# A hybrid decoder block on one core: 208 gathered tokens instead of 192, and other buffers around them

## The chip, the cores and the metric

The kernel runs on one core of one Trainium2 chip. The time is the device time of one execution in microseconds. PE is TensorE (PEld its weight loads), DVE is VectorE, ACT is ScalarE, POOL is GpSimd, SP is SyncE, whose queue issues the plain transfers; POOL issues the indirect ones (row gathers).

## The reference

512 tokens of width 2048 pass a mixer (projections, a short convolution, attention, two merges, an output projection), and then a feed-forward layer of 16384 experts. Each token has 8 heads; a head scores two tables of 128 keys, keeps 16 of each, and picks 16 of the 256 sums. So a token uses 128 of the 16384 experts:

```
hidden = jnp.einsum("td,thkd->thk", xb, u_table[ib])
act = jax.nn.gelu(hidden, approximate=False) * gb
out = jnp.einsum("thk,thkd->td", act, v_table[ib])
```

`u_table` and `v_table` have 16384 rows of 2048 fp32 numbers. Everything is fp32.

## The kernel before, in words

A matmul is done as three fp32r matmuls (`mm3`, lines 161 to 163): each operand is split in a high part (ACT, line 130) and the rest (DVE, line 131). Weights come in halves of 128x1024: `whalf` loads a raw half with SP (512 KB), ACT makes `whi`, DVE makes `wlo`. There are 1024 such halves. Each is used for 24 matmuls in the projections.

The feed-forward layer is done in two ways at once. The first `G0` = 192 tokens are **gathered**: for each of a token's 128 experts POOL fetches a row of `u` and later one of `v` for 128 partitions at a time (1 MB), and DVE multiplies the row with the normalized tokens `gx` and sums (line 701), or multiplies it with the activation and adds it to a sum (line 708). Tokens 0 to 127 are one segment of 128 slots; tokens 128 to 191 are put on the partitions twice, 64 slots each, and the two sums are added at the end. The other `ND` = 320 tokens are **dense**: all experts are computed for them on PE, with 320 columns per matmul, and the result of `u` is multiplied with a plane of gates (`gd`, `gt`) that is zero where a token did not pick the expert. The planes are made of one-hot rows by fp32 matmuls (`gates`, line 673), 16 tokens to a plane.

Order of the program: mixer and output projection of tokens 0 to 255 (until about 690 us); six projections of the second half; the queries of tokens 0 to 255 (`queries`); the rest of the second half's mixer, its output projection and its queries, until about 1705 us; then the dense stage. That has 16 chunks of 8 tiles: `up` (8 units of 48 matmuls with `uT`) and `down` (the same number with `vT`). `up` of chunks 0 to 7 comes first (`AHEAD`), to 2231 us, its results are kept in DRAM (`hdd`); `down` of chunks 0 to 7 follows, to 2690 us; then `up` and `down` alternate.

`route` (the top-16 searches, DVE) and `gates` run beside this in small steps: after each unit or half unit a generator is moved on by a cost budget (`SIDE_A0`, `SIDE_A`, `SIDE_D`). The gather is moved on by `pump(rate)`, one fetch and one consumption per round; in the later dense stage the rest of the rounds is spread evenly over the units. A fetch also waits for a mark two evictions back. The order on each engine is then fixed by a scheduler, and DVE, ACT, PE and SP each work strictly in that order. The consuming instructions on DVE are pinned in their order.

Four `row` buffers (8 KB a partition) hold the fetched rows, the sum of the `v` rounds (`acc`) and other things; a row is fetched when one is free. In the dense stage there are 4 raw buffers `wraw`, 3 further raw ones in `spare`, and 3 pairs of split halves (`WHL`). `finish_rows` normalizes the finished tokens: two `Square` activations write their unwanted products to a PSUM tile of the kind `z`, of which the down projection uses both.

## Time and profile before

| | us |
|---|---|
| median of 3 runs | 3613.26 |
| lowest, highest | 3609.4, 3621.5 |
| the profiled execution: its time | 3619.12 |
| the profiled execution: its span | 3617.4 |
| PE busy in the span | 3513.1 |
| DVE busy | 2831.2 |
| ACT busy | 1616.3 |

The span runs from the first to the last instruction; the execution's time is 1.7 us longer. A matmul's busy time overlaps the next one's, so PE's pace is read from counts of matmuls in a stretch. DMA share is the mean busy share of the 16 DMA engines.

### The profile page before, as it was taken

To read this page: it belongs to the slowest core of one execution; us is meant where nothing else is said; L and a number is where in the kernel's file an instruction comes from. 1 tells how busy PE (TensorE), PEld (TensorE's weight loads), DVE (VectorE), ACT (ScalarE), POOL (GpSimd) and SP (SyncE) were. 2 spreads that over 40 slices of the span, in tenths; PEclk is the share of its full clock that TensorE was granted. 3 is DMA by queue.
4 is the path that set the end of the run, shared out by engine and by line. 5 is a ranking of instruction groups with operands and counts; after the bars stand their busy time and mean duration, and the time that the engine had idled before them with its cause. 6 is when DMAs were issued, how large, how long until landed. Compare 5 with 4: busy or idle time off the path is not lost.

```text
span 3617.4 us, 63262 instructions
## 1 busy us (share of the span) xinstructions
PE 3513.1 (97%) x25347; PEld 3410.4 (94%) x25347; DVE 2831.2 (78%) x4022; ACT 1616.3 (45%) x2275; POOL 659.3 (18%) x520
## 2 busy tenths in 40 slices
PE   9999999999999999889999999999999999999998
PEld 8999998898888999779999999999999999999998
DVE  6565557559987878788999886888887878888886
ACT  6454445445555534544337773333333333333334
POOL 0000000001233322112131111221122322322220
PEclk9999999999999999999999999999999999999999
DMA  6556555654788889898888889899988988899884
GB/s 204 180 178 225 187 187 196 208 184 137 260 348 309 335 332 346 322 331 335 298 327 319 311 315 365 329 356 338 339 328 328 346 330 333 327 346 343 328 329 162
DMA packets 292920, 1049.29 MB, mean 290 GB/s; under 512 B 35921, under 2 KB 105169, under 8 KB 238673
## 3 DMA queue, kind: packets, MB, share of 16 engines
q1 hardware_dynamic: 237328, 642.56, 50.5%
q0 software_dynamic: 55296, 402.68, 28.7%
q8 instruction: 199, 3.26, 0.4%
q14 instruction: 97, 0.79, 0.1%
HBM read 996.57 MB, written 47.97 MB: 289 GB/s over the span
## 4 chain that ended last, share of the span: by engine, by line
PE 59%; DMA 5%; DVE 4%; issue 2%; ACT 1%; POOL 0%; SPq 0%; ACTq 0%; DVEq 0%; POOLq 0%
PE pj L163 10%; PE pj L161 10%; PE pj L162 10%; PE z L161 9%; PE z L162 9%; PE z L163 9%; DVE wlo L131 2%; DMA wraw<-in_w_in 2%; PE pj L673 2%; DMA row<-in_u,idx 1%; DVE row L701 1%; ACT whi L130 1%; PE z L439 1%; DMA row<-in_v,idx 0%; DMA wraw<-in_w_mix 0%
## 5 line engine op out<-in xcount | busy, mean ns | idle before, releaser
L130 ACT ACTIVATE whi<-wraw 128x1024 fp32r<-128x1024 f32 x827 | 874.1, 1059 | 1258.0 <-PE pj L162 723.2
L131 DVE TENSOR_TENSOR wlo<-wraw,whi 128x1024 fp32r<-128x1024 f32 x827 | 1008.3, 1223 | 412.5 <-ACT whi L130 405.6
L161 PE MATMUL pj<-xhi,whi 128*128 128x256 f32 x2560 | 723.5, 283 | 12.5 <-ACT whi L130 10.3
L163 PE MATMUL pj<-xhi,wlo 128*128 128x256 f32 x2560 | 720.4, 283 | 13.5 <-DVE wlo L131 13.4
L162 PE MATMUL pj<-xlo,whi 128*128 128x256 f32 x2560 | 718.1, 281 | 0.0
L161 PE MATMUL pj<-dxhi,whi 128*128 128x320 f32 (+1 forms) x2304 | 710.0, 308 | 4.5 <-ACT whi L130 4.3
L163 PE MATMUL pj<-dxhi,wlo 128*128 128x320 f32 (+1 forms) x2304 | 703.6, 307 | 3.4 <-DVE wlo L131 3.3
L162 PE MATMUL pj<-dxlo,whi 128*128 128x320 f32 (+1 forms) x2304 | 705.2, 306 | 0.0
L161 PE MATMUL z<-ahi,whi 128*128 128x320 f32 x2048 | 632.0, 310 | 3.9 <-ACT z L190 2.9
L162 PE MATMUL z<-alo,whi 128*128 128x320 f32 x2048 | 631.8, 309 | 2.4 <-DVE alo L131 2.4
L163 PE MATMUL z<-ahi,wlo 128*128 128x320 f32 x2048 | 630.6, 309 | 1.8 <-DVE wlo L131 1.8
L163 PEld LDWEIGHTS pj<-xhi,wlo 128*128 128x128 f32 x2560 | 481.6, 189 | 23.6 <-DVE wlo L131 20.9
L161 PEld LDWEIGHTS pj<-xhi,whi 128*128 128x128 f32 x2560 | 482.5, 188 | 21.1 <-ACT whi L130 14.4
L690 POOL DMA_INDIRECT row<-in_v,idx x192 | 292.7, 1525 | 1060.2 <-DVE row L708 429.8
L162 PEld LDWEIGHTS pj<-xlo,whi 128*128 128x128 f32 x2560 | 482.3, 188 | 2.8 <-issue 1.6
L708 DVE SCALAR_TENSOR_TENSOR row<-row,gact 128x2048 f32<-128x2048 f32 x192 | 450.3, 2345 | 27.2 <-DMA row<-in_v,idx 27.2
L701 DVE SCALAR_TENSOR_TENSOR row<-row,gx 128x2048 f32<-128x2048 f32 x192 | 438.3, 2286 | 31.2 <-DMA row<-in_u,idx 31.1
L690 POOL DMA_INDIRECT row<-in_u,idx x192 | 289.0, 1505 | 863.1 <-DVE row L701 239.9
L161 PEld LDWEIGHTS pj<-dxhi,whi 128*128 128x128 f32 x2304 | 434.3, 189 | 5.5 <-ACT whi L130 5.1
L163 PEld LDWEIGHTS pj<-dxhi,wlo 128*128 128x128 f32 x2304 | 432.9, 188 | 5.4 <-DVE wlo L131 5.4
L162 PEld LDWEIGHTS pj<-dxlo,whi 128*128 128x128 f32 x2304 | 434.0, 188 | 0.0
L130 ACT ACTIVATE whi<-spare 128x1024 fp32r<-128x1024 f32 x197 | 208.8, 1060 | 425.4 <-PE z L162 266.9
(232 smaller groups left out, 4979.8 us busy)
## 6 DMA issues: line engine op xcount, KB each, us to landing
wraw<-in_w_in SPq DMA_DIRECT2D x320, 512.0 KB
wraw<-in_uT SPq DMA_DIRECT2D x187, 512.0 KB
wraw<-in_vT SPq DMA_DIRECT2D x128, 512.0 KB
spare<-in_vT SPq DMA_DIRECT2D x128, 512.0 KB
spare<-in_uT SPq DMA_DIRECT2D x69, 512.0 KB
wraw<-in_w_mix SPq DMA_DIRECT2D x64, 512.0 KB
wraw<-in_w_out SPq DMA_DIRECT2D x64, 512.0 KB
wraw<-in_wq SPq DMA_DIRECT2D x64, 512.0 KB
```

The lines of the kernel that those rows point to most:

```text
L130: nc.scalar.activation(hi, src, AF.Copy)
L131: nc.vector.tensor_tensor(lo, src, hi.bitcast(F32), OP.subtract)
L161: nc.tensor.matmul(acc, shi, mhi, start=first, stop=False)
L162: nc.tensor.matmul(acc, shi, mlo, start=False, stop=False)
L163: pe_last[0] = nc.tensor.matmul(acc, slo, mhi, start=False, stop=last)
L439: nc.tensor.matmul(z[:, c], stat.bitcast(F32), src[:, c], start=False, stop=True, skip_group_check=True)
L673: behind(nc.tensor.matmul(gp[:, t * P:t * P + P], oh[:, t, 0], oh[:, t, 1], start=True, stop=True))
L690: ins = nc.gpsimd.indirect_dma_start(out=g, out_offset=None, in_=tab, in_offset=bass.IndirectOffsetOnAxis(ap=idx[0:np_, s:s + 1], axis=0))
L701: pin(nc.vector.scalar_tensor_tensor(g, g, 1.0, gx, OP.mult, OP.mult, accum_out=hid[:, s:s + 1]))
L708: pin(nc.vector.scalar_tensor_tensor(acc[0:np_], g, act[:, s:s + 1], acc[0:np_], OP.mult, OP.add))
```

## The change

Three groups of edits. First, `NG2` goes from 64 to 80: 208 tokens are gathered, in three segments (128 tokens of 128 slots; 64 tokens twice with 64 slots; 16 tokens eight times with 16 slots), 416 rounds instead of 384, and the dense stage has 304 columns and 19 gate planes. The copies of a segment are now added in a tree of transfers and additions. Routing is done for four heads at a time, half 0 of tiles 0 and 1 and then half 1, and the gather starts when the first half's indices are there. Second, the sum of the `v` rounds is kept in `gx`: the first round overwrites it, the last writes to its own row buffer, and the residual `x2d` is loaded and added at the end. So no `row` is held through the `v` rounds, but `gx` is not free for the next segment until the last round. Third, in the dense stage 1 instead of 3 `spare` buffers are left for raw halves (5 raw ones in all instead of 7), and a fourth pair `whi4`, `wlo4` is taken for every fourth half. `rms_scale` now squares 8 pieces of 256 into an SBUF tile.

```
-NG2 = 64
+SEGS = ((0, 0, 128), (1, 0, 64), (1, 64, 16))
+NG2 = 80
-SPB2 = 3
+SPB2 = 1
     def whalf(src):
         turns[0] += 1
-        if spare_ok[0] and turns[0] % 2:
+        if spare_ok[0] and turns[0] % 5 == 0:
             raw = spare()
...
-        hi = wp.tile([P, 1024], F32R, name="whi", bufs=WHL)
-        lo = wp.tile([P, 1024], F32R, name="wlo", bufs=WHL)
+        if spare_ok[0] and turns[0] % (WHL + 1) == 0:
+            hi, lo = (late[2].tile([P, 1024], F32R, name=n, bufs=1) for n in ("whi4", "wlo4"))
+        else:
+            hi, lo = (wp.tile([P, 1024], F32R, name=n, bufs=WHL) for n in ("whi", "wlo"))
...
     def rms_scale(pool, x):
-        ss = pool.tile([P, 2], F32, name="ss", bufs=2)
-        for c in range(2):
-            junk = ztile()
-            nc.scalar.activation(junk, x[:, c * 1024:c * 1024 + 1024], AF.Square, accum_out=ss[:, c:c + 1])
-        return rms_inv(ss)
+        ss = pool.tile([P, 8], F32, name="ss", bufs=2)
+        for c in range(8):
+            junk = pool.tile([P, 256], F32, name="junk", bufs=1)
+            nc.scalar.activation(junk, x[:, c * 256:c * 256 + 256], AF.Square, accum_out=ss[:, c:c + 1])
+        nc.vector.tensor_reduce(ss[:, 0:1], ss, AX.X, OP.add)
+        return rms_root(ss)
...
-    def route(pool, tile_no, st):
+    def route(pool, tile_no, hh, st):
...
             if s == 0:
...
-                acc = row()
-                load_acc(acc)
-            pin(nc.vector.scalar_tensor_tensor(acc[0:np_], g, act[:, s:s + 1], acc[0:np_], OP.mult, OP.add))
+                pin(nc.vector.tensor_scalar(gx, g, act[:, 0:1], None, OP.mult))
+                return
+            pin(nc.vector.scalar_tensor_tensor(g if s == nslot - 1 else gx, g, act[:, s:s + 1], gx, OP.mult, OP.add))
...
+        for tile_no, p0, n in SEGS:
+            R = P // n
...
+            def finish(t):
+                m = P // 2
+                while m >= n:
+                    o = row()
+                    nc.sync.dma_start(o[0:m], t[m:2 * m])
+                    nc.vector.tensor_tensor(t[0:m], t[0:m], o[0:m], OP.add)
+                    m //= 2
                 o = row()
-                nc.sync.dma_start(o[0:NG2], t[r * NG2:r * NG2 + NG2])
-                nc.vector.tensor_tensor(t[0:NG2], t[0:NG2], o[0:NG2], OP.add)
+                nc.sync.dma_start(o[0:n], x2d[rows])
+                nc.vector.tensor_tensor(t[0:n], t[0:n], o[0:n], OP.add)
+                finish_rows(t, rows, final_gain())
...
     def routing(h):
-        for tt in range(2):
-            yield from route(rts[0], 2 * h + tt, st)
+        for hh in range(2):
+            for tt in range(2):
+                yield from route(rts[0], 2 * h + tt, hh, st)
...
-        if st["routes"][0] and what != "half":
+        if st["idx"][0] and what != "half":
```

Place one is DVE in the queries of the first 256 tokens. Before, when half of the scores are searched (`MAX`, `MAX_INDEX`, `MATCH_REPLACE`), twelve `wlo` subtractions follow with nothing between them, and then the next scores:

```order
L550 MATCH_REPLACE ttmp<-ls,row 128x128 x2
L551 MAX ls<-ttmp 128x8 x2
L552 MAX_INDEX ls<-ls,ttmp 128x8 x2
L131 TENSOR_TENSOR wlo<-wraw,whi 128x1024 x12
L548 MAX ls<-row 128x8 x8
```

Now the rest of the routing of four heads stands between the same subtractions (`sv` are the picked sums, `gate` the gates of tile 0):

```order
L133 TENSOR_TENSOR wlo<-wraw,whi 128x1024
L558 MATCH_REPLACE ttmp<-ls,row 128x128
L622 TENSOR_TENSOR spare<-fa,iota 128x1024
L617 TENSOR_SCALAR f_8839<-f_8839 128x64
L558 MATCH_REPLACE ttmp<-ls,row 128x128
L559 MAX ls<-ttmp 128x8
L133 TENSOR_TENSOR wlo<-wraw,whi 128x1024
L624 TENSOR_TENSOR spare<-spare,tif 128x1024
L618 TENSOR_TENSOR fb<-fb,f_8839 128x64
```

Half of two tiles' routing has moved ahead of the scores of the other half; the first consumption of a gathered row stands behind 268 subtractions instead of 289.

Place two is the end of the first segment, tokens 0 to 127, in the dense stage. On DVE, before, the root's steps (L194, L196) have other work between them:

```order
L708 SCALAR_TENSOR_TENSOR row<-row,gact 128x2048
L131 TENSOR_TENSOR wlo<-spare,whi 128x1024
L779 TENSOR_TENSOR hd<-hd,gt 128x320
L194 TENSOR_TENSOR ss<-ss 128x1
L131 TENSOR_TENSOR alo<-hd,ahi 128x320
L196 RECIPROCAL ss<-ss 128x1
L730 SCALAR_TENSOR_TENSOR row<-row,ss 128x2048
L131 TENSOR_TENSOR wlo<-wraw,whi 128x1024
```

Now the residual is added first (L779), and the steps stand closer:

```order
L721 SCALAR_TENSOR_TENSOR row<-row,gact,gx 128x2048
L859 TENSOR_TENSOR dacc<-z,dacc 128x608
L779 TENSOR_TENSOR row<-row 128x2048
L133 TENSOR_TENSOR wlo_28253<-wraw,whi_28252 128x1024
L859 TENSOR_TENSOR dacc<-z,dacc 128x608
L195 TENSOR_REDUCE ss<-ss 128x1
L204 RECIPROCAL ss<-ss 128x1
L746 SCALAR_TENSOR_TENSOR row<-row,ss 128x2048
L795 TENSOR_TENSOR hb<-hb,gt 128x304
L859 TENSOR_TENSOR dacc<-z,dacc 128x608
L133 TENSOR_TENSOR wlo<-wraw,whi 128x1024
```

The place moved from behind 787 subtractions (where `up` of chunk 8 ends and its `down` begins) to behind 747, in the `down` of chunk 6, where the results kept in DRAM are read back beside it (`hb`).

Place three is SP at the end. Now the three transfers of the last segment's tree stand between the last weight loads (before there was one, with 64 rows), and the dense tokens' residual (L903) comes behind the last of them:

```order
L774 DMA row<-row 64x2048
L147 DMA wraw<-in_vT 128x1024 x2
L774 DMA row<-row 32x2048
L147 DMA spare<-in_vT 128x1024
L774 DMA row<-row 16x2048
L778 DMA row<-x2d 16x2048
L740 DMA row<-in_norm_final 128x2048
L147 DMA wraw<-in_vT 128x1024 x2
L740 DMA row<-in_norm_final 128x2048
L147 DMA wraw<-in_vT 128x1024
```

Each of the three waits for the addition before it on DVE, and the loads behind it in the queue wait too.

## Rows read from the trace of the kernel before

**Rows 1.** The page: span and busy time; DMA queues with MB and share.

```profile
span 3617.4 us, 63262 instructions
PE 3513.1 (97%) x25347; PEld 3410.4 (94%) x25347; DVE 2831.2 (78%) x4022; ACT 1616.3 (45%) x2275; POOL 659.3 (18%) x520
q1 hardware_dynamic: 237328, 642.56, 50.5%
q0 software_dynamic: 55296, 402.68, 28.7%
```

**Rows 2.** Busy time by stretch: us, engines with instructions, clock, DMA share, GB/s.

```profile
400.00:500.00 100.00, 100.00 (x851) 100.00 (x850) 57.72 (x72) 42.86 (x53) 0.00 (x0) 1.00 0.56 185
730.00:807.00 77.00, 77.00 (x659) 77.00 (x659) 40.10 (x90) 32.08 (x42) 0.00 (x0) 1.00 0.53 176
1202.00:1277.00 75.00, 74.00 (x617) 72.01 (x616) 60.22 (x63) 34.02 (x42) 21.11 (x14) 1.00 0.95 356
1705.00:2231.00 526.00, 516.84 (x3606) 513.09 (x3605) 459.40 (x1001) 289.62 (x534) 95.38 (x64) 0.99 0.88 322
2231.00:2690.00 459.00, 453.82 (x3076) 450.93 (x3075) 391.85 (x369) 159.57 (x186) 93.36 (x65) 1.00 0.91 338
2690.00:2810.00 120.00, 117.14 (x781) 116.87 (x780) 93.91 (x86) 44.35 (x55) 27.45 (x19) 0.97 0.86 322
2810.00:3541.00 731.00, 730.97 (x4981) 730.28 (x4981) 601.51 (x547) 261.02 (x322) 194.52 (x118) 1.00 0.89 335
3000.00:3100.00 100.00, 100.00 (x684) 100.00 (x683) 78.35 (x82) 34.55 (x44) 25.72 (x16) 1.00 0.86 326
```

**Rows 3.** Groups of the stretch 2810 to 3541 us: busy, mean ns, idle before.

```profile
L162 PEld LDWEIGHTS pj<-dxlo,whi 128*128 128x128 f32 x892 | 167.6, 188 | 0.0
L708 DVE SCALAR_TENSOR_TENSOR row<-row,gact 128x2048 f32<-128x2048 f32 x64 | 150.1, 2346 | 0.0
L701 DVE SCALAR_TENSOR_TENSOR row<-row,gx 128x2048 f32<-128x2048 f32 x57 | 129.9, 2285 | 0.9 <-DMA row<-in_u,idx 0.9
L131 DVE TENSOR_TENSOR wlo<-wraw,whi 128x1024 fp32r<-128x1024 f32 x104 | 127.1, 1222 | 63.9 <-ACT whi L130 62.5 <-issue 0.3
L131 DVE TENSOR_TENSOR alo<-hd,ahi 128x320 fp32r<-128x320 f32 x55 | 26.7, 485 | 1.6 <-ACT ahi L130 1.6
```

**Rows 4.** Waits: 2810 to 3480, 2230 to 2700 and 2690 to 2810 us.

```profile
ACT whi L130 <- PE z L162: 223.2, 86, 5.0
...
POOL row L690 <- DVE row L708: 234.6, 47, 10.1
...
PE z L161 <- ACT z L190: 2.9, 1, 2.9
```

**Rows 5.** The chain that ended last: pieces with start, us, what.

```profile
1271.91 12.69 DMA wraw<-in_w_in
1463.27 15.79 DMA wraw<-in_w_mix
1499.85 0.89 PE pj L673 x8
2747.74 1.16 ACT z L190 x2
```

**Rows 6.** DMA share in tenths and GB/s, 40 slices of 1005 to 1202 us.

```profile
DMA  9999948883999999589938899977393999968984
GB/s 415 420 415 413 415 190 321 309 327 137 319 348 423 421 411 345 221 311 357 358 151 315 293 404 428 417 293 262 122 373 131 334 329 423 399 249 310 340 300 132
```

**Rows 7.** One line's instructions: the squares of 256 columns on ACT.

```profile
L852 ACT ACTIVATE hd<-row x24: 400/403/420, 3554.3 to 3604.8; 128x256 f32<-128x256 f32 x16, 64x256 f32<-64x256 f32 x8
L852 ACT ACTIVATION_READ_ACCUMULATOR hd<-row x24: 185/187/188, 3554.6 to 3605.1; 128x1 f32 x16, 64x1 f32 x8
```

**Rows 8.** DVE's timeline at the end: start, us, what.

```profile
3537.34 2.28 DVE L763 TENSOR_TENSOR row<-row 64x2048 f32<-64x2048 f32 x1
3602.16 0.82 DVE L843 TENSOR_TENSOR dacc<-z,dacc 128x640 f32<-128x640 f32 x1 [1.40 <-PE z L163]
```

More of the change, by code (lines that the diff above doesn't have):

```diff
@@ new lines, in route @@
+            nc.vector.tensor_reduce(eg[:, s, hs], oh, AX.X, OP.add)
+            yield 3.5
+        flat = eg.rearrange("p s a b -> p s (a b)")
+        fs = slice(64 * hh, 64 * hh + 64)
+        if tile_no * P < G0:
+            ef = pool.tile([P, 64], F32, name="fa", bufs=1)
+            nc.vector.scalar_tensor_tensor(ef, flat[:, 0, fs], 128.0, flat[:, 1, fs], OP.mult, OP.add)
+            idx = late[1].tile([P, 64], I32, name=f"idx_{hh}", bufs=2)
+            nc.vector.tensor_copy(idx, ef)
+            st["idx"][tile_no].append(idx)
@@ L712, in gather_tile @@
             for s in range(nslot):
+                while s // idx[0].shape[1] >= len(idx):
+                    yield
                 ready.append((tab, s, fetch(a[tab], s)))
@@ L717, in gather_tile @@
         while ready:
+            g = ready[0][2]
             consume(*ready.pop(0))
             yield
-        finish(acc)
+        finish(g)
     def final_gain():
@@ L768, in dense @@
+            yield from gather_tile(late[1], P, n, idx, gate, load_x, finish)
     def dense(pool, st):
@@ L902, in dense @@
                 nc.sync.dma_start(out[G0 + c:G0 + c + n, half * 1024:half * 1024 + 1024], xs)
-    st = {"routes": [None] * 4}
+    st = {"routes": [None] * 4, "eg": [None] * 4, "idx": [[] for _ in range(4)]}
     credit = 0.0
@@ L908, in block_kernel @@
     pumped = [0]
-    rounds = 2 * P + (2 * (P // (P // NG2)) if NG2 else 0)
+    rounds = sum(2 * n for _, _, n in SEGS)
     def pump(rate):
@@ L968, in background @@
             unit += 1
-        due = min(due, 0.0) + (SIDE_A0 if not st["routes"][0] else SIDE_A if unit < GATES_AT else SIDE_G)
+        due = min(due, 0.0) + (SIDE_A0 if not st["idx"][0] else SIDE_A if unit < GATES_AT else SIDE_G)
         while due > 0:
```

126 lines of the change are left out of this document (55 added, 71 removed).

## The prediction

> **What bounds the kernel now.** I read the page first. PE is busy for 97% of the span and DVE for 78%; the transfers take about 80% of the 16 engines' time [rows 1]. An average says little here, so the next view is the busy time by stretch [rows 2]. A clean stretch of 256-column work has 851 matmuls in 100 us, 117.5 ns each; a clean dense stretch with 320 columns has 684, 146.2 ns each. With these paces each stage shows what it loses. From 2810 to 3541 us there are 4981 matmuls, which need 728 of the 731 us: PE sets the time. From 2231 to 2690 us 3072 dense matmuls need 449 of 459 us. From 1705 to 2231 us there are 3072 dense ones (449 us) and 512 of the one-hot kind, 8 in 0.89 us [rows 5], 57 us: 20 of the 526 us are lost. From 2690 to 2810 us 781 matmuls need 114 us, so 6 are lost.
>
> The waits agree: in the late dense stage ACT waits 223 us for PE to give back a `whi` [rows 4]. Split weights stand ready and PE is behind. The second line to see is the cover that is left there. DVE is busy for 601.5 of 731 us (82%), the transfers have a share of 0.89 and move 335 GB/s [rows 2]. So PE can become faster in the dense stage, but not by much before two neighbours are near their limits.
>
> **The change part by part.**
>
> *Dense columns.* 16 chunks x 16 units x 48 = 12288 matmuls go from 320 to 304 columns. Between 256 and 320 columns a column costs (146.2 - 117.5)/64 = 0.448 ns [rows 2], so 16 columns are 7.17 ns and the sum is **-88 us**, if PE stays the bound. The clock granted there is 1.00, the 2.4 GHz level [rows 2]. The Trainium skill ("TensorE: Matmul & The Clock Gate", Step-by-step: what each phase is for) has one column enter per cycle; by that the 16 columns are 6.67 ns and the sum would be -82 us. The measured slope is the price of this kernel, and I keep it.
>
> *Gate planes.* One plane of 16 tokens less: 16 one-hot products, 2 records each, at 0.111 us [rows 5]: **-3.6 us**. They lie in the first part of the dense stage, where PE works to 98%.
>
> *Before the dense stage.* Routing starts earlier and in halves, and the gather starts some 13 units earlier, so by the order of the calls 18 more rounds (137 instead of 119) are behind when the dense stage begins. These are 42 us of DVE work at 2.3 us each [rows 3]; cutting each routing operation of 128x128 into two of 128x64 adds, at an estimated 0.1 us for each of some 80 more instructions, 8 us. The order (place one) puts about 27 us of routing into the stretch where twelve subtractions stood alone: DVE was busy for only 40.1 of 77 us there [rows 2], so that part is hidden. The other 22 us go where PE and DVE have less to spare. The stretch from 1202 to 1277 us has 15 us of idle DVE [rows 2], and by the order it gets most of them. Bounds: 22 us if none of it is hidden, and -5 us if the earlier rounds relieve the later crowded stretch. I take **+8 us**, nearer to the hidden end, since those stretches have DVE time left.
>
> *More gather in the dense stage.* 14 of the 32 added rounds fall here, 281 instead of 267, because the rate is spread over the units. In the late part that is about 1.25 per unit of 48 matmuls instead of 1.17 (121 consumptions in 104 units [rows 3]). DVE's work of a unit goes from 601.5/104 = 5.78 us to 5.78 + 0.08 x 2.3 less 5% of the shorter operations (0.49 us for a 320-column one [rows 3]), about 5.92 us, while the unit shrinks from 7.02 to 48 x 0.139 = 6.67 us: 89% busy. In the part from 2231 us it is 391.85/64 + 0.15 - 0.06 = 6.2 of 6.67 us, 93%; from 1705 us about 465 of 500 us, 93%. At 82% DVE cost PE 0.4%, at 85% (2231 us) it was 2.2%, at 87% with small transfers late (1705 us) 4%. I take 1.2% of 854 us, 4% of 427 us and 26 us, against 3, 10 and 20 now: **+20 us**. Bounds: 0 if the fourth split pair absorbs it, 33 us if all 14 rounds show.
>
> *The `v` sum in `gx`.* In the `v` rounds POOL waited 234.6 us for the row consumed before it, as only three rows were left [rows 4]; now four are. DVE did not wait in that stretch, so nothing is gained on the path. `gx` becomes free later; the order leaves 5 splits between the last round of a segment and the first of the next, time enough. 0 us.
>
> *The squares in SBUF and the end of a segment.* The squares held a `z` buffer and PE waited 2.9 us for them [rows 4, 5]; 6 us were lost around it [rows 2]. That goes. But eight squares take 8 x 0.59 = 4.7 us of ACT [rows 7] instead of 2.4, and by the order (place two) DVE stands at L195 and L204 with one subtraction in front, with three more large operations around. About 11 us pass between two subtractions; four split pairs cover 13 us. Between -6 us and +4 us: **-3 us**.
>
> *Raw buffers.* Seven raw halves were a lead of 7 x 3.5 = 24.6 us, five are 16.7 us. The longest load pieces in the chain are 12.69 and 15.79 us, both from stretches with four raw buffers [rows 5]; in the late dense stage no load ended a wait of the list. The lead still covers a load, and the added split pair gives back 3.3 us. 0 us, with the price of the cover in the rivals.
>
> *The end.* The last segment needs three transfers and four additions of 2.28 us [rows 8] in turn, and the last weight loads stand behind them on SP (place three). Counted from its last round, the last load is issued some 16 us later and is needed after 40 us; the dense residual lands at about 40 us, before PE's transposes block. DVE then has about 22 us of work for a PE that ends 19 us later. **+2 us**, between -3 and +10.
>
> The sum is -88 - 3.6 + 8 + 20 - 3 + 2 = **-65 us**. It is made against the profiled execution: 3619.1 us (a span of 3617.4), 0.16% above the median of 3613.3. Carried to the median it gives **3549 us**.
>
> **The rivals.**
>
> A, *the transfers become the bound.* A late unit moves 335 GB/s x 7.02 us = 2.36 MB; 0.08 rounds more of 1.05 MB (402.68 MB in 384 [rows 1]) make it 2.44 MB, in 6.67 us 366 GB/s. From 2231 us it is 2.47 MB, 371 GB/s. No long stretch shows that: the best is 356 GB/s at a share of 0.95 [rows 2]. If 356 is the limit, a unit takes 6.85 us for the 118 late units with gathers (+21 us) and 6.95 us for the 64 from 2231 us (+18); 10 us of it are in my sum already. That gives -36 us, **3577 us**. Against it: five slices in a row, 25 us, ran at 413 to 420 GB/s [rows 6]. The Trainium skill ("DMA: Bandwidth & Descriptors", Where 436 GB/s comes from) says that for transfers between HBM and SBUF the HBM side, about 358 GB/s a core, binds; by that the time would be close to this rival's. The slices at 420 GB/s speak against it for one core.
>
> B, *DVE becomes the bound.* All of the 22 and 33 us show: -88 - 4 - 3 + 22 + 33 + 2 = -38 us, **3575 us**. For it: 93% in two parts. Against: the work is spread evenly, and ACT, DVE's supplier, has time.
>
> C, *slower.* The same transfers, with the smaller raw cover, can't go beyond the 338 GB/s that the stretch from 2231 us averaged at a share of 0.91. Then the units take 7.22 and 7.31 us, and 65 + 41 us come back, less the 10: +31 us, **3644 us**. It turns the sign where the limit lies below 348 GB/s. The 356 GB/s over 75 us speak against it.
>
> D, *the columns don't matter,* since a weight load takes 188 ns [rows 3], longer than a matmul's 146 ns. Then nothing is gained and 3549 + 88 = **3637 us** come out. But 256 columns ran at 117.5 ns with the same loads.
>
> **How the numbers follow.** The forecast, 3530 to 3560 us: 0.62. A 0.14, B 0.13. A smaller gain still, near no change: 0.03. More than forecast, below 3530 us: 0.03. C 0.04, D 0.01. The likeliest is 3549 us. A range from 3526 to 3582 us takes in A and B and leaves out little more than 1 in 10. A change of 0.3% (11 us) is about what a measurement of this kernel can tell: faster 0.92, same 0.03, slower 0.05.
>
> **What would show it.** A clean late stretch should have about 719 matmuls in 100 us. PE's wait for ACT at the squares should be gone. DVE should be near 89% in the late part, the transfers near 366 GB/s with a share of 0.95 or more. If waits of ACT for `wraw` or `spare` from `in_uT` and `in_vT` appear after 2231 us, it is A or C; if PE waits for `wlo` with the loads on time, it is B. The dense stage should start within 10 us of 1705 us. The prediction is wrong if the dense stage, which now takes 1912 us to the end, is not shorter by 60 us or more.

## The result: 0.5% slower

The changed kernel takes 3628.5 us (median; 3625.0 to 3640.7), the kernel before 3611.8 us beside it: a ratio of 1.0054, 95% interval 1.0029 to 1.0079. The forecast was 3549 us (range 3526 to 3582).

The profiled execution of the changed kernel has a span of 3639.0 us, 21.6 us longer than that of before [rows 1]. It is the slowest of its five executions, 12 us above the median, so up to that much of a difference between its stages and those of another run need not come from an edit. The page, in the order of the earlier rows, and the shares of the chain that ended last:

```profile
span 3639.0 us, 63428 instructions
PE 3461.7 (95%) x25315; PEld 3349.3 (92%) x25315; DVE 2901.7 (80%) x4164; ACT 1628.8 (45%) x2313; POOL 749.9 (21%) x552
q1 hardware_dynamic: 236240, 642.06, 50.0%
q0 software_dynamic: 59904, 436.23, 30.7%
PE 44%; DVE 11%; DMA 11%; issue 11%; POOL 3%; ACT 3%; SPq 0%; ACTq 0%; DVEq 0%; POOLq 0%
```

PE does its work in 51 us less and the program is longer all the same: PE stands idle for 73 us more. The busy time by stretch shows where (us, engines with instructions, clock, DMA share, GB/s; cut where the stages end):

```profile
1202.00:1285.00 83.00, 70.84 (x521) 65.19 (x520) 68.76 (x75) 40.84 (x46) 26.86 (x24) 0.94 0.88 351
1285.00:1740.00 455.00, 414.72 (x3001) 389.86 (x3000) 356.55 (x505) 193.84 (x272) 85.63 (x59) 0.97 0.87 325
1740.00:2246.00 506.00, 494.38 (x3593) 492.00 (x3593) 457.56 (x1000) 291.74 (x535) 98.75 (x64) 0.99 0.88 323
2246.00:2729.00 483.00, 449.41 (x3078) 443.43 (x3077) 399.97 (x393) 164.75 (x208) 136.83 (x69) 0.96 0.91 336
2729.00:3505.00 776.00, 758.29 (x5375) 751.30 (x5374) 663.17 (x607) 282.49 (x358) 235.27 (x140) 1.00 0.94 356
```

Against [rows 2], stage by stage: the work before the dense stage ends 34 us later (1740 in place of 1706). The first eight up chunks take 506 us in place of 526. The first eight down chunks take 483 in place of 459. From there to the same weight half near the end, 776 in place of 795 (2690 to 3485 us). The rest takes 134 in place of 132. That is +34 - 20 + 24 - 19 + 2 = +21 us.

The stretch from 2246 us is the new thing. Its waits (total, times, longest us):

```profile
ACT whi L132 <- PE z L166: 104.3, 45, 8.1
ACT whi L132 <- DMA wraw<-in_vT: 62.8, 28, 14.3
ACT ahi L132 <- DVE hb L795: 60.2, 11, 12.8
ACT ahi L132 <- PE z L167: 56.8, 25, 7.5
...
PEld z L167 <- DVE wlo L133: 31.2, 17, 5.5
```

ACT waits for loads of `in_vT`, and PE's side waits for `wlo`: split weights no longer stand ready. DVE's and ACT's timeline (start, us, what, with its idle time and who ended it) shows one of PE's gaps there, from 2394.2 to 2398.8 us:

```profile
2389.96 4.73 DVE L721 SCALAR_TENSOR_TENSOR gx<-row,gact,gx 128x2048 f32<-128x2048 f32 x2
...
2391.58 1.06 ACT L132 ACTIVATE whi<-wraw 128x1024 fp32r<-128x1024 f32 x1 [6.04 <-DMA wraw<-in_vT]
...
2395.31 2.34 DVE L721 SCALAR_TENSOR_TENSOR gx<-row,gact,gx 128x2048 f32<-128x2048 f32 x1
2397.57 2.35 DVE L133 TENSOR_TENSOR wlo<-wraw,whi 128x1024 fp32r<-128x1024 f32 x2
```

A load was 6 us late for ACT, but its high part was done by 2392.6 us. What PE waited for was DVE, where three rounds of gathering stood ahead of the subtraction that PE needed. Of the six gaps of 2.8 us or more in this stretch, two go back to late transfers (a load that ACT awaited for 14.3 us, rows that DVE awaited for 4.8 us), three to rounds that stand on DVE ahead of a subtraction, like this one, and one to the end of the first segment.

### The profile page after: what moved, and what is told of

Read it like the earlier page. It is cut to its first block, busy times and chain, and to the rows that moved or that the text cites. A ratio compares the mean times of both kernels' runs of the same rounds, so it can differ in the third digit from the quotient of the medians.

```text
span 3639.0 us, 63428 instructions
## 1 busy us (share of the span) xinstructions
PE 3461.7 (95%) x25315; PEld 3349.3 (92%) x25315; DVE 2901.7 (80%) x4164; ACT 1628.8 (45%) x2313; POOL 749.9 (21%) x552
## 4 chain that ended last, share of the span: by engine, by line
PE 44%; DVE 11%; DMA 11%; issue 11%; POOL 3%; ACT 3%; SPq 0%; ACTq 0%; DVEq 0%; POOLq 0%
PE pj L167 10%; PE pj L165 10%; PE pj L166 10%; PE z L167 4%; DVE wlo L133 4%; PE z L165 4%; PE z L166 4%; DMA wraw<-in_vT 3%; POOL row L706 3%; DMA row<-in_u,idx 2%; DVE row L714 2%; PE pj L686 2%; DMA row<-in_v,idx 1%; DMA wraw<-in_uT 1%; DVE gx L721 1%
## 5 line engine op out<-in xcount | busy, mean ns | idle before, releaser
L132 ACT ACTIVATE whi<-wraw 128x1024 fp32r<-128x1024 f32 x946 | 995.7, 1057 | 1306.7 <-PE pj L166 661.7
L133 DVE TENSOR_TENSOR wlo<-wraw,whi 128x1024 fp32r<-128x1024 f32 x946 | 1147.2, 1220 | 335.5 <-ACT whi L132 332.1
L167 PE MATMUL pj<-dxhi,wlo 128*128 128x304 f32 (+1 forms) x2304 | 691.7, 303 | 21.6 <-DVE wlo L133 21.5
L165 PE MATMUL pj<-dxhi,whi 128*128 128x304 f32 (+1 forms) x2304 | 698.2, 304 | 1.2 <-ACT whi L132 1.0
L166 PE MATMUL pj<-dxlo,whi 128*128 128x304 f32 (+1 forms) x2304 | 694.1, 302 | 0.0
L167 PE MATMUL z<-ahi,wlo 128*128 128x304 f32 x2048 | 624.8, 307 | 33.5 <-DVE wlo L133 33.4
L165 PE MATMUL z<-ahi,whi 128*128 128x304 f32 x2048 | 624.0, 306 | 8.8 <-ACT whi L132 8.5
L166 PE MATMUL z<-alo,whi 128*128 128x304 f32 x2048 | 623.8, 305 | 0.0
L721 DVE SCALAR_TENSOR_TENSOR gx<-row,gact,gx 128x2048 f32<-128x2048 f32 x202 | 473.6, 2344 | 22.3 <-DMA row<-in_v,idx 22.0
L167 PEld LDWEIGHTS z<-ahi,wlo 128*128 128x128 f32 x2048 | 389.6, 191 | 40.4 <-DVE wlo L133 40.3
```

What stands on the lines that cost most here:

```text
L132: nc.scalar.activation(hi, src, AF.Copy)
L133: nc.vector.tensor_tensor(lo, src, hi.bitcast(F32), OP.subtract)
L165: nc.tensor.matmul(acc, shi, mhi, start=first, stop=False)
L166: nc.tensor.matmul(acc, shi, mlo, start=False, stop=False)
L167: pe_last[0] = nc.tensor.matmul(acc, slo, mhi, start=False, stop=last)
L721: pin(nc.vector.scalar_tensor_tensor(g if s == nslot - 1 else gx, g, act[:, s:s + 1], gx, OP.mult, OP.add))
```

## The experiments

One table holds all of them. Times of stages are those of the profiled executions. The stages end at the same weight halves in every kernel, and the rounds are the gathered rows that landed in a stage, both counted from the trace's matmuls and packets. "Late" is 5376 matmuls. In the fifth column the time that the transfers' packets took there, as a mean over 16 engines, is divided by what PE needs alone: 752 us with 304 columns (139.9 ns for each matmul, from the stretch of e4 below), 788 us with 320 (146.6 ns, from e9's). Times with their rounds in brackets.

| kernel | to the dense stage | up 0 to 7 | down 0 to 7 | late | transfers / PE in late | ratio to before |
|---|---|---|---|---|---|---|
| before | 1706 (119) | 525 (63) | 459 (65) | 795 (129) | 0.89 | 1 |
| changed | 1740 (137) | 506 (64) | 482 (67) | 776 (139) | 0.97 | 1.0054 |
| e1 seven raw, three split | 1732 (136) | 510 (64) | 461 (68) | 793 (138) | 0.96 | 1.0098 (1.0081 to 1.0115) |
| e2 old routing | 1713 (119) | 513 (65) | 483 (72) | 805 (150) | 1.00 | 1.0075 (1.0057 to 1.0093) |
| e3 before, five raw, four split | 1699 (118) | 524 (65) | 462 (64) | 791 (129) | 0.90 | 0.9996 (0.9986 to 1.0005) |
| e4 two segments | 1734 (137) | 504 (62) | 448 (59) | 753 (119) | 0.90 | 0.9870 (0.9854 to 0.9887) |
| e5 shorter DVE work | 1740 (137) | 495 (63) | 472 (68) | 801 (139) | 0.96 | 1.0069 (1.0046 to 1.0092) |
| e6 shorter transfers | 1743 (137) | 504 (63) | 451 (68) | 762 (139) | 0.94 | 0.9926 (0.9905 to 0.9946) |
| e7 six raw, four split | 1740 (137) | 502 | 469 | 783 | 0.97 | 1.0056 (1.0037 to 1.0076) |
| e8 one more row ahead | 1735 | 506 | 471 | 786 | 0.96 | 1.0090 (1.0069 to 1.0111) |
| e9 320 columns, 384 rounds | 1737 (136) | 516 (63) | 462 (59) | 788 (119) | 0.88 | 1.0079 (1.0062 to 1.0095) |
| e10 320 columns, 416 rounds | 1739 (136) | 513 (64) | 483 (68) | 804 (139) | 0.94 | 1.0247 (1.0229 to 1.0264) |
| e11 later start | 1687 (112) | 512 (65) | 492 (78) | 816 (150) | 1.02 | 1.0123 (1.0106 to 1.0140) |
| e12 planes by chunk | 1732 (137) | 504 (63) | 472 (68) | 774 (139) | 0.96 | 1.0028 (1.0015 to 1.0042) |
| e13 e9 with later start | 1692 (111) | 515 (65) | 469 (66) | 802 (134) | 0.92 | 1.0007 (0.9998 to 1.0016) |
| e14 e13, planes by chunk | 1697 (112) | 516 (65) | 468 (65) | 802 (134) | 0.91 | 1.0008 (0.9999 to 1.0016) |
| e15 before, planes by chunk | 1704 (119) | 522 (63) | 459 (65) | 794 (129) | 0.89 | 1.0006 (0.9998 to 1.0015) |
| e16 more rounds in up | 1734 (137) | 531 (76) | 470 (63) | 780 (131) | 0.95 | 1.0103 (1.0088 to 1.0117) |
| e17 before, 56 stores more | 1752 (119) | 543 (63) | 459 (65) | 795 (129) | 0.90 | 1.0156 (1.0139 to 1.0174) |
| e18 e13, seven raw | 1689 (112) | 524 (64) | 457 (66) | 803 (134) | 0.92 | 1.0007 (0.9998 to 1.0016) |

An edit here often moves other instructions too, since the scheduler then writes another order. Compared position by position, every engine of e12 has the instructions of the changed kernel in the same order; e14 agrees in this way with e13, and e15 with the kernel before. In e5 1093 and in e6 719 of DVE's 4164 positions hold another instruction than in the changed kernel. e9, e10, e13, e14 and e18 also square as the kernel before does, into `z`.

### The raw buffers: e1, e3, e7

```diff
-SPB2 = 1
+SPB2 = 3
-        if spare_ok[0] and turns[0] % 5 == 0:
+        if spare_ok[0] and turns[0] % 2:
...
-            hi, lo = (late[2].tile(...) for n in ("whi4", "wlo4"))
```

e1 is this edit on the changed kernel; e3 is its reverse on the kernel before; e7 has `SPB2 = 2` and each third load in a spare, with the fourth split pair kept.

> The changed kernel with the weight buffers of the kernel before in the dense stage: seven raw halves and three split pairs in place of five and four. Theory R (five raw halves halve the lead of a load, loads land too late, and PE pays at every delay of a load): the stretch from 2246 to 2730 us loses most of its 63 us of ACT waiting for raw halves from in_vT and PE's gaps there (31 us in all), the late stretch loses its 69 us of such waits; 40 to 60 us come back, 3570 to 3590 us. Theory G (the 32 added rounds of gathering fill DVE and the transfers, whatever the buffers): within 10 us of the changed kernel's 3628 us. Theory S (the fourth split pair was worth something): above 3628 us. The part before the dense stage stays the same in all three.

> The kernel before with one edit of the change: five raw halves and four split pairs in the dense stage. Theory R: waits of ACT for raw halves appear from 2231 us, PE gets gaps there, 20 to 60 us slower, 3632 to 3670 us; the price may be smaller than in the changed kernel, since 320 columns leave 5% more time to each load. Theories G and S: within 8 us of 3612 us, or a few us less. Until 2200 us it is the kernel before in all.

> The changed kernel with six raw halves in place of five, and its four split pairs. Theory of two covers (raw halves keep the loads early where down chunks follow each other, split pairs keep PE going past DVE's stalls, and each is worth something where it is missing): the 483 us from 2246 us become 462 to 472 us as with seven raw halves, the late stretch keeps the 776 us that it has with four split pairs: 3605 to 3620 us. If the 21 us that seven raw halves gave there came from something else (the turn of the buffers, not their number), 3628 us.

e1's two long stretches:

```profile
2241.00:2702.00 461.00, 440.11 (x3075) 433.98 (x3074) 397.84 (x386) 162.98 (x204) 142.08 (x69) 0.99 0.94 349
2702.00:3495.00 793.00, 765.25 (x5380) 761.01 (x5379) 658.00 (x605) 288.49 (x359) 233.44 (x138) 0.99 0.92 347
```

Seven raw halves give back 21 us in the down chunks, as theory R has it. With its three split pairs it then loses 17 us in the late stage and some at the end, and its median, 3646.4 us, is 18 us above the changed kernel's, so R's sum falls. e3 is within 0.1% of before: with 320 columns and 384 rounds the two buffer plans are worth the same. e7 gains 13 us in the down chunks and loses 7 late, and is 8 us slower in all (3636.9 us). The buffers, with the order that comes with them, move the loss about; no number of them tried here takes it away.

### Whose time the rounds take: e4, e5, e6

e4 drops `(1, 64, 16)` from `SEGS`, so 16 tokens are computed by nobody. e5 and e6 keep all 416 rounds and cut one side of each by an eighth from the dense stage on:

```diff
+            cc = slice(0, 1792 if dense_on[0] else D)
-pin(nc.vector.scalar_tensor_tensor(g, g, 1.0, gx, ...))
+pin(nc.vector.scalar_tensor_tensor(g[:, cc], g[:, cc], 1.0, gx[:, cc], ...))
```

is e5 (the `v` sum alike), and e6 gathers rows of 1792 numbers into `g[:, 0:1792]`. To keep DVE at 2048 columns, e6 has it multiply `gx` with itself in the `u` rounds and read the first 1024 columns of a row twice in the `v` rounds; a round takes 2284 and 2346 ns as before and still waits for its row.

> The changed kernel without the third gathered segment: tokens 192 to 207 are gathered by nobody and their rows are not written; 384 rounds of gathering as before, 304 columns. Theory G (the 32 rounds are what costs): 50 us or more come back, 3560 to 3580 us. Theory R: the raw cover still is short, so the rounds give back only their own transfers and DVE time, 10 to 25 us, 3603 to 3618 us. In both the part before the dense stage keeps its 1745 us or loses a few, as the rate of gathering there is the same.

> The changed kernel, but from the dense stage on DVE works on 1792 of the 2048 columns of each gathered row (the sums of products leave out the last 256 columns; the transfers stay whole). With 281 rounds there and about 0.29 us less for each it takes off 81 us of DVE's work, about what the 34 rounds took off that the kernel with two segments had less in the dense stage, and none of the transfers. Theory V (DVE's work is what the added rounds cost): most of the 62 us that two segments gave back come here too, 3566 to 3590 us. Theory T (the transfers are what they cost): 3615 to 3628 us.

> The changed kernel, but from the dense stage on each gathered row is 1792 numbers long in place of 2048 (taken from other places of the tables, so the gathered sums are of other numbers), and DVE works on 2048 columns as before. It takes off 37 MB of transfers, about what 34 rounds of 1.05 MB have, and none of DVE's work. Theory T: 3566 to 3590 us. Theory V: 3615 to 3628 us. If both share the price, the two kernels come out between, and their gains add up to about 62 us.

e4's down and late stretches (the late one from 2793 us):

```profile
2238.00:2685.00 447.00, 436.02 (x3069) 432.63 (x3068) 377.94 (x369) 162.42 (x205) 119.65 (x61) 0.99 0.92 339
...
2793.00:3439.00 646.00, 644.65 (x4608) 643.68 (x4607) 528.50 (x488) 235.77 (x290) 166.48 (x104) 1.00 0.90 335
```

The same stretches of e5:

```profile
2234.00:2706.00 472.00, 447.09 (x3074) 441.39 (x3073) 382.14 (x391) 164.44 (x207) 119.23 (x69) 0.97 0.93 343
2706.00:3507.00 801.00, 769.97 (x5381) 766.25 (x5380) 627.77 (x607) 280.80 (x359) 215.51 (x140) 0.98 0.90 345
```

And of e6:

```profile
2246.00:2698.00 452.00, 438.76 (x3079) 433.44 (x3078) 399.08 (x394) 163.45 (x208) 138.65 (x69) 0.99 0.94 340
2698.00:3460.00 762.00, 755.29 (x5378) 751.68 (x5377) 660.32 (x607) 283.04 (x359) 251.86 (x140) 1.00 0.92 339
```

The third segment costs 62 us (3628.5 - 3566.5). In the profiled executions, 73 us apart, 34 lie in the down chunks and 23 late. In e4's late stretch PE does 4608 matmuls in 644.65 of 646 us: the columns are worth what was forecast, when nothing else binds. Taking the transfers' share of that load off (e6) gives back 39 us; taking DVE's share off (e5) makes the kernel 14 us slower. e5 gains some 10 us each in the up and the down chunks and loses 25 late. In the sum that is T and not V, and in the up chunks it is the other way: e5 gains there, e6 doesn't. But both have another order on DVE than the changed kernel, and in e5 the order has a price of its own.

Why e5 loses late is seen in DVE's timeline at one of six gaps of 3.7 us, some 113 us apart:

```profile
2893.24 0.79 DVE L861 TENSOR_TENSOR dacc<-z,dacc 128x608 f32<-128x608 f32 x1 [2.82 <-PE z L168]
2893.95 2.02 DVE L716 SCALAR_TENSOR_TENSOR row<-row,gx 128x1792 f32<-128x1792 f32 x1
...
2895.89 2.36 DVE L133 TENSOR_TENSOR wlo<-wraw,whi 128x1024 fp32r<-128x1024 f32 x2
```

DVE waits for PE's last product, and PE's next subtraction stands on DVE behind that wait and a round. PE then waits for the sum and the round whole. It is a wait of each for the other that the written order makes. In e5 the six are 22 us, with the clock at 1.2 GHz for 3.4 or 6.8 us after each; e1 has six such gaps too, of 1.7 to 4.0 us. The late stages of e4 and e9 have none. So e5 does not show that DVE's work is free: less these gaps and the clock behind them its late stage would be some 10 us shorter than the changed kernel's (an estimate from these rows).

### One more row ahead: e8

`DEPTH = 2` in place of 1.

> The changed kernel with one more gathered row asked for ahead of the row that is consumed (a depth of 2 in place of 1), which the four free rows allow. DVE's waits for rows from in_u and in_v (67 us in all) shrink. Theory W (subtractions for PE stand behind DVE's waits for late rows, so these waits cost PE time, before the dense stage and in it): 10 to 30 us come back, part of it before 1740 us. Theory V: DVE waits less but its work stays, 0 to 8 us come back. If POOL, which now has no row to spare, gets the wait instead, nothing comes back.

The kernel is 17 us slower than the changed one (3645.8 us). In its profiled execution 5 us are gained before the dense stage and 11 in the down chunks, and 10 are lost late. DVE's waits for rows fell from 67 to 26 us, so theory W falls: they are not what the change costs.

### Before the dense stage: e2, e11

e2 puts back `route` for eight heads; e11 keeps the halves and has only

```diff
-        if st["idx"][0] and what != "half":
+        if st["routes"][0] and what != "half":
```

and the same condition for `SIDE_A0`.

> The changed kernel with the routing of the kernel before: a token tile is routed for all eight heads at once, and the gather starts only when tile 0 is routed whole; the last gather rows of tile 1 are cut from the one index tile. Theory P (halved routing and the earlier gather cost the time before the dense stage): the first dense matmul comes at about 1715 us in place of 1745, and, since some 18 rounds go back into the dense stage, at most 10 us of the 30 are lost there: 3600 to 3612 us. Theory P2 (the rounds cost the same wherever they lie): the dense stage starts 25 to 30 us earlier and is as much longer, 3620 to 3635 us. If the 30 us come from elsewhere, the dense stage still starts at about 1740 us.

> The changed kernel, routing in halves, but the gather and the lower rate of the side work start only when all eight heads of tile 0 are routed, as in the kernel before. Theory PE (the early gather costs the time before the dense stage: its transfers and DVE work come among the routing): the dense stage starts at 1710 to 1720 us in place of 1740 to 1745, and the rounds go into the dense stage, 3625 to 3640 us in all. Theory PH (the routing in halves costs it: more and shorter instructions on DVE): the dense stage still starts after 1730 us.

e11's first stretches:

```profile
1202.00:1285.00 83.00, 81.52 (x686) 80.87 (x685) 68.15 (x74) 34.51 (x44) 14.44 (x12) 1.00 0.93 341
1285.00:1687.00 402.00, 372.98 (x2705) 350.65 (x2704) 321.11 (x466) 176.79 (x250) 74.26 (x53) 0.97 0.90 332
```

From 1202 us PE is busy for 81.5 of 83 us, in the changed kernel for 70.8. The early gather puts 25 rounds ahead of the dense stage (137 in place of 112) and they cost 53 us, 2.1 us each; that the halves of routing are no cost is shown by e11 against e2 (1687 and 1713, with 7 rounds fewer). PE's waits say by whom. In the kernel before from 1202 to 1710 us and in the changed kernel from 1202 to 1745 us (total, times, longest):

```profile
PE pj L163 <- DVE wlo L131: 6.5, 8, 2.3
...
PE pj L167 <- DVE wlo L133: 21.5, 16, 3.6
...
PE z L166 <- DVE wlo L133: 6.0, 4, 2.1
```

In e11, from 1202 to 1690 us:

```profile
PE pj L167 <- DVE wlo L133: 6.0, 7, 1.4
...
PE z L166 <- DVE wlo L133: 2.6, 2, 1.4
```

But e11 and e2 are slower in all (3654.3 and 3642.1 us): the rounds they put off cost more later (150 in the late stage, 805 and 816 us). Theory P2 holds in kind; both times lie above the ranges that were expected for it, so a round cost more late than before the dense stage.

### Four corners: e9, e10

`NG2 = 64` with two segments (e9), and with the third one gathered for nothing (e10).

> The changed kernel's program with the sizes of the kernel before: 192 gathered tokens, two segments (384 rounds), 320 dense columns; the squares as before the change, for room. It is the fourth corner of a square: 304 columns with 416 rounds took 3628 us, 304 with 384 took 3566. Theory P: it has the 28 us before the dense stage, gets back about half in the first eight up chunks, as the changed kernel did, and has PE as its bound from there: 3615 to 3635 us. Without a price of the earlier part: 3600 to 3612 us. Columns at 0.44 ns for each of 12288 matmuls, 86 us at most, stand against 3566 us: up to 3650 us.

> As the kernel with 320 columns and two segments, but the third segment of 16 tokens is gathered too, for nothing: its sum is worked out and not stored. Theory T (the transfers' engines are the bound only where PE's unit is short: with 320 columns a unit gives them 5% more time, and 730 us of engine time in 795 us is a share of 0.92): the 32 rounds cost 0 to 25 us over the kernel with two segments. If 32 rounds have a price of their own, whatever PE does: about 60 us over it. From the four corners it follows that the 16 columns are worth 80 us with 384 rounds and, by theory T, 10 to 40 us with 416.

e9's late stretch, then e10's:

```profile
2715.00:3504.00 789.00, 789.00 (x5382) 789.00 (x5381) 623.29 (x576) 282.55 (x339) 229.89 (x120) 1.00 0.87 320
```

```profile
2735.00:3539.00 804.00, 793.06 (x5380) 791.05 (x5379) 669.78 (x609) 283.67 (x347) 244.72 (x140) 0.99 0.92 345
```

With 320 columns the 32 rounds cost 21 us in the down chunks, 15 late and 29 after the late stage, where e10 takes 161 us and e9 132; with 304, 34 and 23. The sum, 64 us, is what was expected if the rounds have a price of their own, and T allowed 25 at most. PE's waits in e10 from 2735 us to the end, and ACT's longest from 3539 us on, show what the 64 are made of:

```profile
PE z L165 <- ACT z L194: 37.4, 2, 27.4
PE pj L167 <- DVE wlo L133: 0.9, 5, 0.2
...
ACT z L194 <- DVE row L781: 23.0, 1, 23.0
```

PE waits twice, 10.0 us late and 27.4 us near the end, for ACT to give back the `z` that the squares took, and ACT waits for the sum at the end of a segment; the three transfers of the third segment's tree come before the longer one. The changed kernel squares into SBUF and has no such wait. Without these 37 us some 27 are left, 21 of them in the down chunks, and late the 32 rounds cost PE nothing else: it waits 0.9 us for `wlo`. So a faster PE makes the same rounds dearer, as T has it. In e9 most of the price of the earlier start remains (31 us at the dense stage, 19 at its weight half near the end) and 7.7 us of waiting for `z` come in the down chunks, so it is slower than the kernel before with the same columns and rounds.

### Small packets, and where rounds could go: e12 to e18

```diff
-    gd = dram.tile([NB, P, P, 16], F32, name="gd")
+    gd = dram.tile([P, NE, NB, CHUNK, 16], F32, name="gd")
...
-            nc.sync.dma_start(gt, gd[:, :, ch * CHUNK:ch * CHUNK + CHUNK].rearrange("b p e t -> p b e t"))
+            nc.sync.dma_start(gt, gd[:, ch])
```

is the edit of e12 (on the changed kernel), e14 (on e13) and e15 (on the kernel before).

> The changed kernel with the gate planes kept in DRAM by chunk: a load of gate planes then reads 9.7 KB in a row for each partition in place of 19 pieces of 512 bytes, and the store writes pieces of 512 bytes in place of 8 KB. The small packets took a share of 0.077 of the engines' time from 2246 to 2729 us and 0.041 after it for 1.2 MB a chunk; in long packets the same bytes need about two thirds of that time. Theory T (engine time of the transfers is the bound): the stretch from 2246 us gets shorter by 5 to 12 us and the late one by 5 to 12 us; the part up to 2246 us loses 0 to 10 us by its stores: 3605 to 3622 us. If the bytes, not the engines' time, are the bound: 3628 us, within 8.

> The kernel before with the gate planes kept in DRAM by chunk and no other edit. In its late stage PE is the bound, so nothing comes back there; the stretches up to 2690 us lose 20 and 10 us now. Theory T: 2 to 8 us less than the kernel before. If the late loads of gate planes or the stores in short pieces come in the way: 0 to 5 us more.

> 192 gathered tokens, two segments and 320 dense columns as in the kernel before, with the changed program's routing in halves, its sum in the tile of the normalized tokens and its weight buffers, but the gather starts when all eight heads of tile 0 are routed; the squares as before the change. Theory L (a round costs about 2 us where the transfers or DVE are full, wherever it lies, and the late dense stage with 320 columns still takes some 135 rounds within PE's time): the dense stage starts at 1685 to 1695 us in place of 1737, most of these 45 us are kept, since the late stage grows only from 789 to 795 us and the one from 2253 us by some 10: 3595 to 3612 us, less than the kernel before. If the rounds cost their 2 us there too: 3630 to 3640 us.

> The same with the gate planes kept in DRAM by chunk. Theory L and T: it loses less from 2250 us on and in the first part of the dense stage, 5 to 10 us less than without: 3588 to 3606 us, faster than both kernels. If the small packets cost nothing where PE is the bound, the same time as without, within 5 us.

> The kernel with 192 gathered tokens, 320 columns, routing in halves and the gather started by the whole of tile 0, now with the weight buffers of the kernel before (seven raw halves, three split pairs). It was 24 us ahead of the kernel before at 2231 us and gave 10 us back from there to 2690 us and 7 after it, with 66 and 134 rounds in place of 65 and 129. Theory: the lead of the loads was what it lacked from 2231 us, so 5 to 10 us are kept there: 3600 to 3612 us. If the rounds moved to the later stages take back what the earlier ones gained, whatever the buffers: within 5 us of 3615 us.

e12 is 7 us below the changed kernel's 3628.5 (3621.6), at the edge of what the runs can tell, 10 us of it in the down chunks. There the packets' time falls by 15 us, with the order on every engine unchanged: the one test on the changed kernel in which nothing but the transfers differs, and it is worth a part of the down chunks' loss. On the kernel before and on e13, where the transfers have slack, the same edit does nothing.

e13 is 24 us ahead of the kernel before when the down chunks begin and 7 ahead after the late stage; at the end nothing is left. e18 gets 12 us back in the down chunks and has lost 9 in the up chunks, where only the written order differs: 3616.7 us, the same. It is not the rounds put off that take the lead back after 2690 us. PE's longest waits from there on, in the kernel before, e13 and e18:

```profile
PE z L161 <- ACT z L190: 2.9, 1, 2.9
...
PE z L165 <- ACT z L194: 11.4, 2, 8.0
...
PE z L163 <- ACT z L192: 16.7, 2, 8.6
```

These are the squares in `z` again, now behind the added sum at the end of a segment. With the 2.9 us of the kernel before, e18 would come to about 3603 us and e13 to about 3606, both inside the ranges expected of a gain (an estimate; no run has the late start, 320 columns and the squares in SBUF together). No version here that computes the whole reference beats the kernel before.

e16 has `RATE_W = 1.2`.

> The changed kernel with 1.2 rounds of gathering a unit in place of 1.0 in the first eight up chunks, some 13 to 24 rounds more there and as many fewer after 2246 us. Theory L: the late stage gets below the 128 rounds that it takes within PE's time and comes to 755 to 762 us, the down chunks of the first half get shorter by 10 to 15 us, but DVE, 458 of 506 us busy in the up chunks, has no time left there and that stage gets longer by 20 to 40 us: 3615 to 3635 us in all. If the up chunks have room (the share of the transfers is 0.88 there), 3590 to 3605 us.

Twelve more rounds in the up chunks make them 25 us longer, 2.1 us each, where DVE was 90% busy; the down chunks get back 12, and the late stage nothing: 3649.8 us, above both ranges. The late stage did not come down to 755 to 762 us with 131 rounds in place of 139; its order differs too, so what the eight rounds alone are worth is not shown.

e17, the last, adds transfers and no work on PE, ACT or DVE:

```diff
+            if what is None and 128 <= unit < 240 and unit % 2 == 0:
+                nc.sync.dma_start(junkd[unit // 2 % 8], st["dense_x"][0][:, 0:3].bitcast(F32))
```

> The kernel before, with 56 stores of 1.97 MB... that is 128 partitions x 3840 bytes, 0.49 MB each, of the normalized tokens to a scratch place in DRAM that nobody reads, one in each second unit of the late dense stage (2690 to 3480 us); nothing else is changed, no engine but SP has an instruction more. Each takes the 16 engines about 1.2 us, worked out from the 159 ns of a packet of 4096 bytes; 67 us in all, so that the transfers' time there goes from 703 to 770 us of the 789 that PE needs. Theory T (the late stage loses by the transfers' time as a share of PE's, about nothing at 0.90, 20 to 40 us at 0.96 to 0.97): 20 to 45 us slower than the kernel before, 3633 to 3658 us, all of it after 2690 us. If DVE's work or the order of its instructions made the loss of the changed kernel's late stage: 3613 to 3621 us.

Each store is of 0.49 MB. They wait for nothing but the tile, and SP issued all 56 from 1600 to 1726 us, not in the late stage; so the run does not test what it was made for, and 3671.7 us is not the price of transfers late. It does price 67 us of engine time in a crowded place, with the weight loads behind the stores in SP's queue: 46 of the 65 us are lost before the dense stage and the rest by 2018 us of the kernel before (the weight half of 2459 us comes at 2524, and the distance stays). The stretches of e17 from 1600 us:

```profile
1600.00:1700.00 100.00, 80.58 (x558) 76.43 (x558) 64.99 (x124) 28.91 (x37) 12.70 (x11) 0.88 1.02 415
1700.00:1760.00 60.00, 49.91 (x338) 47.87 (x339) 34.25 (x41) 19.09 (x23) 10.22 (x6) 0.89 0.97 384
```

## Why the prediction was wrong

The forecast was 65 us below the kernel before, the profiled execution is 22 above it. Of these 87 us some 42 belong to the gather in the dense stage, 26 to the part before it and 6 to the columns.

*Dense columns, -88 us:* right in kind. 146.6 ns (e9) against 139.9 (e4) are 6.7 ns for 16 columns, 82 us in all; rival D is out. The prediction took its 7.17 ns from the slope between 256 and 320 columns. The Trainium skill ("TensorE: Matmul & The Clock Gate", Step-by-step: what each phase is for) has one column enter per cycle; the 6.67 ns that the prediction worked out from it and set aside agree with these runs.

*More gather in the dense stage, +20 us (0 to 33):* **the step that failed.** The prediction sized it by DVE's busy share, some 6 to 7 us more in each of the three parts, and put the lack of room for the transfers at nothing beyond that. At 6.7 ns a matmul the columns are worth 20.6 us in the up chunks (3072 matmuls), 20.6 in the down chunks and 36 in the late stage. Measured were -20, +24 and -19: next to nothing was lost in the up chunks, 45 us in the down chunks and 17 late, 62 us. The down chunks have 67 rounds in place of 65: it is not more gather that costs there, but the same gather in a shorter unit.

e4 and e6 show that fewer rounds or shorter transfers give most of the 62 us back, and e12 that lighter transfers give some back with the order held. How much of it is the transfers' alone stays open. Sorted by the table's fifth column, late stages with 304 columns end 1 us over what PE needs at 0.90, 10 us at 0.94, 22 to 49 us at 0.95 to 0.97, 53 and 64 us at 1.00 and 1.02. Those with 320 columns, at 0.88 to 0.94, end 0 to 16 us over, nearly all of it PE's wait for the squares in `z` (2.9 us before, 8.0 to 10.0 in e10, e13, e14 and e18) and the lower clock after it. DVE's busy time sorts the 304-column stages nearly as well (615 us in e4, 647 to 663 in those 22 to 41 over, 687 and 693 in e2 and e11), but for e5, 628 us and 49 over, and e6, 660 and 10 over. These two have DVE's order changed, and e5's order costs 22 us and the clock after its gaps. Nearly every wait of PE late in the changed kernel ends at a `wlo` of DVE. So rival B, DVE as the bound, isn't excluded; what the runs show is that DVE's share by itself did not give the size.

In the down chunks 19 us come by the clock: the granted clock is 0.96, PE is busy for 449.4 us, and 3072 matmuls at 139.9 ns need 430.

*Rival A* named the resource that e6 and e12 point to and priced it too low, by a limit of 356 GB/s and the slices at 413 to 420 GB/s as evidence against it. Those slices stand beside a 9 in the row of shares [rows 6]: all engines were busy there. It is what the engines gave when full. e17 had such a share for 100 us, and PE was busy for 80.6 of them; the longer stretches of these runs end at 0.94. A number to forecast was the share: 0.89 [rows 2], times 7.02 / 6.72 for the shorter unit (48 matmuls of 139.9 ns) and 2.44 / 2.36 for the added bytes, is 0.96 of PE's new unit. The rule of the Trainium skill on which A leaned ("DMA: Bandwidth & Descriptors", Where 436 GB/s comes from), some 358 GB/s a core on the HBM side, is not what bound: e17 moved 415 GB/s for 100 us at a share of 1.02.

*Rival C*, 3644 us, came nearest in the sum. Its 338 GB/s is what the down chunks moved (336), but the late stage moved 356, and the raw cover that it blamed is not enough: e1 has seven raw halves and is slower still.

*Before the dense stage, +8 us (-5 to 22):* wrong in size, 34 us in the profiled execution and 26 to 31 in e1, e4 and e9. The term took idle DVE time as room. The rounds cost 2.1 us each, near DVE's 2.3 us, and PE's wait there is for `wlo`: a round stands ahead of the subtraction that PE needs. That reading rests on the waits; no run cut DVE's work before the dense stage.

*Raw buffers, 0 us:* right in the sum (e1, e3, e7), for a reason that was partly wrong. From issue to use a load had 22.2 us late in the kernel before and 11.9 in the changed one (medians, from the trace's issues and packets), not 24.6 and 16.7, and loads did come late in the down chunks; seven raw halves gain 21 us there and lose 17 late with three split pairs.

*Squares and the end, -3 and +2 us:* PE's wait for ACT at the squares is gone from 2690 us on; the end takes 2 us more. *The `v` sum in `gx`, 0 us:* its free row bought nothing (e8); it was not undone by itself, nor was the gate plane's -3.6 us.

Of the signs that the prediction set, both came: ACT's waits for `wraw` from `in_vT`, which spoke for A or C, and PE's waits for `wlo`, which spoke for B. From 3000 to 3100 us the changed kernel did 686 matmuls, not 719, with 353 GB/s at 0.93:

```profile
3000.00:3100.00 100.00, 96.87 (x686) 95.64 (x685) 83.31 (x71) 33.79 (x41) 30.81 (x18) 1.00 0.93 353
```

The dense stage takes 1899 us to the end in place of 1912, 13 us less and not 60.

## What to carry to other kernels

Price added transfers as the share of the DMA engines' time that the new, shorter unit will need, not in GB/s against a burst. Here the late stage with 304 columns lost 1 us at 0.90, 10 at 0.94 and 22 or more from 0.95 on. Where PE, DVE and the transfers are all near 0.9, a gain on one is paid out of the others: a round cost 2.1 us of PE's time before the dense stage and in the up chunks, and those that e2 and e11 put off cost more late. To learn which of two engines an operation is dear on, shorten the operation on one of them alone, and see whether the order of instructions stayed: where it did not, the order can be what was measured. Before a loss is laid to the thing that was moved, read what PE waited for: in five runs here it was an old buffer of the squares.

## What the runs showed of the hardware

Packets have a floor that goes with their size. For 4096 bytes it was 156 to 159 ns in every stretch read, at shares from 0.53 to 1.02. Counted from the trace's packets of the changed kernel, 2246 to 2729 us:

```
queue, bytes   packets   mean ns   lowest 5%   share of 16 engines
q1  4096        16648      174        159         0.375
q0  8192         8632      331        309         0.369
q1   512        19456       30         27         0.077
q1  1216         7203       57         53         0.053
```

16 engines at 159 ns for 4096 bytes are 412 GB/s, at 309 ns for 8192 bytes 424, at 27 ns for 512 bytes 303. Crowding did not lengthen packets: the mean for 4096 bytes was 196 ns from 300 to 500 us of the kernel before, at a share of 0.60, and 161 ns from 1600 to 1700 us of e17, at 1.02. The delay of a load is outside its packets: from issue to its last semaphore count it took 5.7 us in the down chunks of the kernel before and 8.6 in those of the changed one (medians), 9.2 and 15.6 for the slowest tenth.

Short gaps on PE cost more than their length: the granted clock falls to 0.5, the 1.2 GHz level, for 3.4 or 6.8 us after each of the changed kernel's eight gaps of 3 to 5 us. The trace of the changed kernel has 24 falls to that level, that of the kernel before 9.
